# A transformer layer in float32 on one Trainium2 core: pool waits by tile, memory loads behind the first values, one more side block in front, query weights behind the last head

## The chip, the cores and the metric

The kernel runs on one core of one Trainium2 chip. The metric is the time of one execution in microseconds of the device (us); the time before is the median of three runs. The engines are named as the profile names them: PE (TensorE matmul), PEld (its weight loads), DVE (VectorE), ACT (ScalarE), POOL (GpSimd) and SP (SyncE, which here only issues DMAs).

## The reference

One layer over 1024 tokens of width 1024, with 256 memory tokens, in three residual steps. Norms are RMS norms.

```python
def parallel_mixer(xn, w_in, ...):
    proj = xn @ w_in
    fq, fk, fv, ff, gq, gk, gv, glr, gr = jnp.split(proj, _split_points(), axis=-1)
    ...
    fox_out = fox_attention(fq, fk, fv, log_f).reshape(B, S, FOX_WIDTH)      # 8 heads of 64
    ...
    return jnp.concatenate([fox_out, gla_out], axis=-1) @ w_out

def memory_cross_attention(hn, memn, wq, wkv, q_norm_g, k_norm_g, wo):       # 4 heads of 256
    q = rms_norm((hn @ wq).reshape(B, S, XATTN_HEADS, XATTN_HEAD_DIM), q_norm_g)
    k, v = jnp.split(memn @ wkv, 2, axis=-1)
    ...

h = h + parallel_mixer(rms_norm(h, norm_mix_g), ...)
h = h + memory_cross_attention(rms_norm(h, norm_xattn_g), rms_norm(mem, norm_mem_g), ...)
h = h + (jnp.square(jax.nn.relu(rms_norm(h, norm_mlp_g) @ mlp_w1))) @ mlp_w2
```

The forgetting attention (fox) is causal softmax attention over 8 heads with a bias from the running sum of log forget gates.

## The kernel before

Matrices are multiplied as two rounded parts each: a product is three matmuls (high times high, high times low, low times high), and `gemm` issues these three for each slice of 128 rows. `evac_split` makes the two parts of a PSUM bank: ACT writes the high part, DVE subtracts it for the low part. `wsplit` loads two slices of weights at a time into a `raw` tile (512 KB) and splits them, ACT for the high part `wh`, DVE for the low part `wl`.

The layer runs in stages. `mixer_inputs` makes the projections; its last loop makes the fox values, splits them and stores them tile by tile in DRAM (`vd`, L600). `fox` is the stage that the change touches. For each of 8 heads it loads the values of the head (`va`, L723), and for each of four pairs of query tiles `fox_scores` makes scores (`s`), a row maximum on DVE (`nm`), an exponential on ACT (`p`), a reciprocal on DVE (`rrec`) and a scaling on POOL (L671). `values` then transposes `p` in groups of up to four squares into one of three PSUM banks `tr` (L696), splits each group into `pth` (ACT) and `ptl` (DVE), and adds the products with the values into the one bank `pv` (L704). At the end of a pair `ol` (ACT, L707) and an add into `mixf` (DVE, L710) empty that bank. `fox_prep` loads the queries and keys of the next head (`qa`, `ka`, `qb`, `kb`).

Between these pieces a generator, `side_work`, puts work that depends on no head: eight blocks of the output projection's part for the gated linear attention (`out_part`: 12 matmuls into the one bank `mm`, then DVE adds the residual, `t2k`, L817, and stores it in `hpd`), the splitting of the memory's columns (`memr`, from `memT`), keys and values of the memory from the weights `wkv`, and eight blocks more of the output projection. `step` decides how many side pieces follow each pair of query tiles: 26 over the 32 pairs, after one ahead of the first. Then `project_out` ends the output projection, and `xattn` begins with the query weights (`weights(0)`, from `wq`).

A scheduler orders each engine's instructions from the dependencies and its own estimate of time, so a line's place in the program is a wish and not a place in a queue. `issue_after` adds a dependency: what is written under it is issued behind the named instruction. Each engine, SP too, works through its own instructions in order, so a waiting one holds those behind it. A DMA is issued with one of eight semaphores (`DMAHW0` to `DMAHW7`) in turn, and must wait until the earlier DMA of that semaphore has landed.

Pools reuse memory. A pool that is opened where another has been closed waits, at its first tile, for everything that used the memory before. With `reuse_waits="tile"` each tile waits only for what used the bytes of that tile. In `fox`, `foxpt` (the tiles `pth` and `ptl`) and `foxol` (`ol`) lie where the staging tiles `qn` of the values' loop lay.

Of the kernel before, what the change touches and what calls it, by code (L numbers as in the profile page):

```python
# [21 lines left out]
AF = mybir.ActivationFunctionType  # L22
ALU = mybir.AluOpType
# [7 lines left out]
P = 128  # L31
# [16 lines left out]
def f(ap):  # L48
    return ap.bitcast(F32)


class Layer:
# [52 lines left out]
    def gemm(self, ps, lh, ll, rh, rl, start=True, stop=True, **kw):  # L105

        mm = self.nc.tensor.matmul
        n = len(lh)
        for k in range(n):
            mm(ps, lh[k], rh[k], start=start and k == 0, stop=False, **kw)  # L110
            mm(ps, lh[k], rl[k], start=False, stop=False, **kw)  # L111
            mm(ps, ll[k], rh[k], start=False, stop=stop and k == n - 1, **kw)  # L112

# [564 lines left out]
    def fox(self):  # L678
        nc = self.nc
        with ExitStack() as st:  # L680
            pt = self.open(st, "foxpt", 5)
            olp = self.open(st, "foxol", 3)
            mmp = self.open(st, "mm2", 1, space=PSUM)
            pvp = self.open(st, "pv2", 1, space=PSUM)
            trp = self.open(st, "tr2", 3, space=PSUM)

            def values(h, sb, pp, A):
                va = A[4]
                pv = self.T(pvp, [P, 256], F32, "pv")
                for b in range(sb + 1):  # L690
# [10 lines left out]
                    self.evac_split(th[:, 0:n * P], tl[:, 0:n * P], tp[:, 0:n * P])  # L701
                    for j, w in ((0, th), (1, th), (1, tl), (0, tl)):
                        js = slice(j * 256, min((j + 1) * 256, n * P))
                        nc.tensor.matmul(pv[:, 256 - (js.stop - js.start):256], va[:, 2 * b + j, :], w[:, js],  # L704
                                         start=b == j == 0 and w is th, stop=b == sb and j == 0 and w is tl)
                ol = self.T(olp, [64, 256], F32, "ol")
                nc.scalar.activation(ol, pv[64:128, :], AF.Copy)  # L707
                o = self.mixf[(h % 2) * 64:(h % 2) * 64 + 64, 2 * sb:2 * sb + 2, h // 2, :]
                v3 = lambda ap: ap.rearrange("p (a b) -> p a b", a=2)
                nc.vector.tensor_tensor(o, v3(pv[0:64, :]), v3(ol), ALU.add)  # L710
                return first

            side = self.side_work(self.side, mmp, trp)
            prep = self.fox_prep
            next(side)
            A = self.fox_first

            def step(s):
                for _ in range(((s + 1) * 26 + 8) // 32 - (s * 26 + 8) // 32):
                    next(side, None)  # L720

            for h in range(8):
                nc.sync.dma_start(f(A[4]), self.vd[:, h])  # L723
                for g in range(2):
# [14 lines left out]
    def side_work(self, mp, mmp, trp):  # L739
# [11 lines left out]
        for t in range(2):  # L751
            xt = self.T(mp, [P, 4, M], F32, "memr", bufs=2)
            nc.sync.dma_start(xt, self.memT[:, 4 * t:4 * t + 4, :])
            for j in range(4):
                k, c = 4 * t + j, slice(2 * (j % 2), 2 * (j % 2) + 2)
                self.evac_split(mh[k // 2][:, c, :], ml[k // 2][:, c, :], xt[:, j, :].rearrange("p (t s) -> p t s", t=2), gm[:, k:k + 1])
            yield
# [4 lines left out]
        for n in range(4):  # L762
            W = self.wsplit(self.wkv[:, n * 512:(n + 1) * 512], None, rooms=mp)
            if n == 0:
# [34 lines left out]
    def out_part(self, mp, mmp, n, ks):  # L799
# [7 lines left out]
        for half in range(2):  # L807
# [3 lines left out]
            for i in range(4):  # L811
                ps = self.T(mmp, [P, 512], F32, "mm")
                c = slice(i * P, (i + 1) * P)
                self.gemm(ps, *([w[:, c] for w in w_] for w_ in W), *A)
                xt = self.T(mp, [P, 512], F32, "t2k", bufs=3)
# [154 lines left out]
    def xattn(self):  # L970
        nc = self.nc
        with ExitStack() as st:
# [16 lines left out]
            def weights(n):  # L989
                Ws[n] = self.wsplit(self.wq[:, n * 512:(n + 1) * 512], C_XAT)  # L990
                kT = self.T(kvp[n], [P, 2, 4, M], F32R, "kT")
# [367 lines left out]
```

## Time and profile before

| what | value |
|---|---|
| time, median of 3 runs | 1440.09 us (1438.77 to 1441.18) |
| the profiled execution | 1440.62 us |
| its span, first to last instruction | 1438.9 us |
| mean granted clock of PE | 0.998 |
| busy: PE, DVE, ACT, POOL | 99%, 65%, 47%, 27% of the span |
| DMA | 223.91 MB, mean 156 GB/s |
| the fox stage | about 325 to 550 us of the span |

A row of time has a start, a duration, engine, line, operation and tiles (out<-in); "xN" merges N neighbours of one kind, and a bracket gives the engine's idle time before the row and what ended it. A row of windows has the stretch, its length, busy time and count of PE, PEld, DVE, ACT and POOL, the granted clock, the share of DMA in use and GB/s. A row of waits reads: who waited for whom, us in total, times, longest.

### The profile page before, as it was taken

The numbers are of one execution on the slowest core, as the hardware profiler recorded it, in microseconds if no ns is written. First come the engines' busy times: TensorE is split into PE (matmuls) and PEld (weight loads), VectorE is DVE, ScalarE is ACT, GpSimd is POOL, SyncE is SP. The second block draws the span as 40 slices with busy tenths as digits, with TensorE's granted clock in tenths as the row PEclk, the third lists the DMA queues.
The fourth block names the chain that finished last, engine by engine and source line by source line (L and its number), as shares of the span: only waits on it lengthen the run. The fifth ranks groups of instructions, "written<-read, shape, count | busy, mean of one in ns | idle before, by whom it ended". The sixth has DMA issues, their size and how long they took to land.

```text
span 1438.9 us, 19147 instructions
## 1 busy us (share of the span) xinstructions
PE 1421.3 (99%) x7036; PEld 1185.4 (82%) x7036; DVE 937.8 (65%) x1342; ACT 675.2 (47%) x1095; POOL 385.2 (27%) x404
## 2 busy tenths in 40 slices
PE   9999999999999999999999999999999999999998
PEld 7788788887888887888888888888888888888887
DVE  5366732437887766666545895656556968778797
ACT  3544441336777655454532364444546745335230
POOL 3235423311333223412212300000000552233454
PEclk9999999999999999999999999999999999999999
DMA  8335530278678634322573124344446835436353
GB/s 313 92 65 140 130 79 0 74 190 285 173 193 239 177 110 148 124 74 90 171 273 140 44 95 179 145 168 190 176 175 231 320 107 190 134 133 217 123 191 124
DMA packets 121164, 223.91 MB, mean 156 GB/s; under 512 B 8912, under 2 KB 54512, under 8 KB 118512
## 3 DMA queue, kind: packets, MB, share of 16 engines
q1 hardware_dynamic: 119776, 218.25, 46.6%
q10 hardware_dynamic: 1296, 4.46, 1.0%
q8 instruction: 55, 0.90, 0.2%
q14 instruction: 37, 0.30, 0.1%
HBM read 150.59 MB, written 72.09 MB: 155 GB/s over the span
## 4 chain that ended last, share of the span: by engine, by line
PE 89%; DMA 4%; ACT 3%; DVE 2%; issue 2%; POOL 0%; SPq 0%; ACTq 0%; DVEq 0%; POOLq 0%
PE mm L110 15%; PE mm L111 15%; PE mm L112 15%; PE my L110 7%; PE my L112 7%; PE my L111 7%; PE tr L112 3%; PE tr L111 3%; PE tr L110 3%; PE pv L704 2%; PE tr L696 2%; PE s L660 1%; PE s L661 1%; DMA ud<-h 1%; DMA raw<-in_mlp_w_dram 1%
## 5 line engine op out<-in xcount | busy, mean ns | idle before, releaser
L110 PE MATMUL my<-x,g 128*128 128x512 f32 x464 | 180.7, 390 | 0.5 <-ACT h L1295 0.3
L111 PE MATMUL my<-x,g 128*128 128x512 f32 x464 | 180.6, 389 | 0.0
L112 PE MATMUL my<-x,g 128*128 128x512 f32 x464 | 180.5, 389 | 0.0
L111 PE MATMUL mm<-wl,xh 128*128 128x512 f32 x320 | 126.5, 396 | 0.6 <-DVE wl L100 0.6
L110 PE MATMUL mm<-wh,xh 128*128 128x512 f32 x320 | 125.9, 396 | 0.5 <-ACT wh L99 0.4
L112 PE MATMUL mm<-wh,xl 128*128 128x512 f32 x320 | 125.7, 393 | 0.0
L1087 ACT ACTIVATE g<-s 128x1024 fp32r<-128x1024 f32 (+1 forms) x72 | 69.0, 964 | 101.1 <-PE my L112 41.1
L1088 DVE TENSOR_TENSOR g<-raw,g 128x512 fp32r<-128x512 f32 (+3 forms) x72 | 69.2, 965 | 69.8 <-ACT g L1087 69.7
L1087 ACT ACTIVATE g<-raw 128x512 fp32r<-128x512 f32 (+3 forms) x72 | 55.5, 773 | 102.4 <-DMA raw<-in_mlp_w_dram 39.6
L110 PEld LDWEIGHTS my<-x,g 128*128 128x128 f32 x464 | 87.1, 188 | 19.5 <-ACT h L1295 0.7
L111 PEld LDWEIGHTS my<-x,g 128*128 128x128 f32 x464 | 87.1, 188 | 18.3 <-DVE x L1088 0.2
L1114 POOL TENSOR_TENSOR s<-raw 128x384 f32<-128x384 f32 (+1 forms) x20 | 26.5, 1324 | 282.1 <-DMA raw<-in_mlp_w_dram 254.5
L112 PEld LDWEIGHTS my<-x,g 128*128 128x128 f32 x464 | 87.1, 188 | 17.9
L671 POOL TENSOR_SCALAR p<-p,rrec 128x128 f32<-128x128 f32 (+3 forms) x64 | 52.8, 831 | 151.6 <-DVE rrec L670 143.1
L1088 DVE TENSOR_TENSOR g<-s,g 128x1024 fp32r<-128x1024 f32 (+1 forms) x72 | 86.6, 1205 | 9.0 <-ACT g L1087 9.0
L1257 DVE TENSOR_TENSOR x<-x 128x1024 fp32r<-128x1024 f32 (+1 forms) x64 | 77.0, 1223 | 17.6 <-ACT x L1256 17.3
L111 PE MATMUL mm<-x,g 128*128 128x512 f32 x220 | 85.7, 389 | 0.0
L110 PE MATMUL mm<-x,g 128*128 128x512 f32 x220 | 85.6, 389 | 0.0
L112 PE MATMUL mm<-x,g 128*128 128x512 f32 x220 | 85.6, 389 | 0.0
L110 PE MATMUL tr<-x,g 128*128 128x512 f32 x212 | 82.5, 389 | 0.0
L111 PE MATMUL tr<-x,g 128*128 128x512 f32 x212 | 82.5, 389 | 0.0
L112 PE MATMUL tr<-x,g 128*128 128x512 f32 x212 | 82.5, 389 | 0.0
(316 smaller groups left out, 3665.8 us busy)
## 6 DMA issues: line engine op xcount, KB each, us to landing
ud<-h SPq DMA_DIRECT2D x32, 768.0 KB
x<-ud SPq DMA_DIRECT2D x48, 512.0 KB
raw<-in_mlp_w_dram SPq DMA_DIRECT2D x20, 1024.0 KB
raw<-in_mlp_w_dram SPq DMA_DIRECT2D x16, 768.0 KB
raw<-in_w_in_dram SPq DMA_DIRECT2D x23, 512.0 KB
raw<-in_xattn_wkv_dram SPq DMA_DIRECT2D x16, 512.0 KB
od<-o SPq DMA_DIRECT2D x32, 256.0 KB
ud<-h SPq DMA_DIRECT2D x32, 256.0 KB
```

The lines of the kernel that those rows point to most:

```text
L110: mm(ps, lh[k], rh[k], start=start and k == 0, stop=False, **kw)
L111: mm(ps, lh[k], rl[k], start=False, stop=False, **kw)
L112: mm(ps, ll[k], rh[k], start=False, stop=stop and k == n - 1, **kw)
L660: nc.tensor.matmul(ps[:, c], qa[:, ts], ka[:, c], start=True, stop=False)
L661: nc.tensor.matmul(ps[:, c], qb[0:68, ts], kb[0:68, c], start=False, stop=not last)
L671: nc.gpsimd.tensor_scalar(p[:, 0:n], p[:, 0:n], rr, 1.0, ALU.mult, ALU.mult)
L696: t = nc.tensor.transpose(tp[:, c * P:(c + 1) * P], pp[i][:, (2 * b + j) * P:(2 * b + j + 1) * P], self.ident)
L704: nc.tensor.matmul(pv[:, 256 - (js.stop - js.start):256], va[:, 2 * b + j, :], w[:, js], start=b == j == 0 and w is th, stop=b == sb and j ...
L1087: a = self.nc.scalar.activation(hi, src, AF.Copy)
L1088: d = self.nc.vector.tensor_tensor(lo, src, f(hi), ALU.subtract)
L1114: eng.tensor_tensor(s[:, 0], raw[:, 3], raw[:, 2], ALU.add)
L1257: nc.vector.tensor_tensor(lo, f(lo), f(hi), ALU.subtract)
```

## The change

Four edits. `foxpt` waits by tile, and it is opened behind `foxol` instead of ahead of it. The loads of the memory's columns and of `wkv` are issued behind the load of the first head's values. Two pieces of side work instead of one are issued ahead of the heads, 25 instead of 26 follow with them, and the first head's first products with the values are issued behind the last matmul of the second side block. The loads and the splitting of the first query weights are written to be issued behind the last head's two closing instructions.

```diff
@@ gemm
-            mm(ps, ll[k], rh[k], start=False, stop=stop and k == n - 1, **kw)
+            end = mm(ps, ll[k], rh[k], start=False, stop=stop and k == n - 1, **kw)
+        return end.ins
@@ fox
-            pt = self.open(st, "foxpt", 5)
             olp = self.open(st, "foxol", 3)
+            pt = self.open(st, "foxpt", 5, reuse_waits="tile")
...
-                    for j, w in ((0, th), (1, th), (1, tl), (0, tl)):
...
+                    with ExitStack() as behind:
+                        if h == sb == 0:
+                            behind.enter_context(self.tc.issue_after(self.side_end))
+                        for j, w in ((0, th), (1, th), (1, tl), (0, tl)):
...
-                nc.scalar.activation(ol, pv[64:128, :], AF.Copy)
+                end = nc.scalar.activation(ol, pv[64:128, :], AF.Copy).ins
...
-                nc.vector.tensor_tensor(o, v3(pv[0:64, :]), v3(ol), ALU.add)
+                self.fox_end = end, nc.vector.tensor_tensor(o, v3(pv[0:64, :]), v3(ol), ALU.add).ins
...
-            next(side)
+
+            for _ in range(2):
+                next(side)
...
-                for _ in range(((s + 1) * 26 + 8) // 32 - (s * 26 + 8) // 32):
+                for _ in range(((s + 1) * 25 + 8) // 32 - (s * 25 + 8) // 32):
                     next(side, None)
...
-                nc.sync.dma_start(f(A[4]), self.vd[:, h])
+                self.va_load = nc.sync.dma_start(f(A[4]), self.vd[:, h]).ins
+                if h == 0:
+                    self.va_first = self.va_load
@@ side_work
-            nc.sync.dma_start(xt, self.memT[:, 4 * t:4 * t + 4, :])
+            with self.tc.issue_after(self.va_first):
+                nc.sync.dma_start(xt, self.memT[:, 4 * t:4 * t + 4, :])
...
-            W = self.wsplit(self.wkv[:, n * 512:(n + 1) * 512], None, rooms=mp)
+            with self.tc.issue_after(self.va_first):
+                W = self.wsplit(self.wkv[:, n * 512:(n + 1) * 512], None, rooms=mp)
@@ out_part
-                self.gemm(ps, *([w[:, c] for w in w_] for w_ in W), *A)
+                self.side_end = self.gemm(ps, *([w[:, c] for w in w_] for w_ in W), *A)
@@ xattn, weights(n)
-                Ws[n] = self.wsplit(self.wq[:, n * 512:(n + 1) * 512], C_XAT)
+
+                with self.tc.issue_after(self.fox_end[0]), self.tc.issue_after(self.fox_end[1]):
+                    Ws[n] = self.wsplit(self.wq[:, n * 512:(n + 1) * 512], C_XAT)
```

How it moves instructions, at three places. First ACT, at the first `pth` of the first head, with the semaphores that each instruction waits for; before:

```order
L668 ACTIVATE p_550_2952,rsum_2953<-s_548_2944,nm_2950 128x896 [waits DVE_49]
L117 ACTIVATE pth_2862<-tr_2858 128x384 [waits DMAHW6_49,PE_49,DMAHW7_49,Activation_49,Pool_49]
L117 ACTIVATE pth_2896<-tr_2891 128x512 [waits PE_49]
L117 ACTIVATE pth_2909<-tr_2904 128x512 [waits PE_49]
L668 ACTIVATE p_555_2964,rsum_2965<-s_553_2958,nm_2962 128x512 [waits DVE_49,Pool_49]
L117 ACTIVATE pth_2921<-tr_2917 128x384 [waits PE_49]
L88 ACTIVATE wh_3738<-raw_783_3736 128x512 [waits DMAHW1_49]
L88 ACTIVATE wh_3742<-raw_783_3736 128x512
L88 ACTIVATE wh_3748<-raw_3746 128x512 [waits DMAHW0_49]
L88 ACTIVATE wh_3752<-raw_3746 128x512
```

and in the changed kernel, where lines stand one or ten further down:

```order
L669 ACTIVATE p_552_2969,rsum_2970<-s_550_2961,nm_2967 128x896 [waits DVE_49]
L118 ACTIVATE pth_2879<-tr_2875 128x384 [waits PE_49,Activation_49,Pool_49]
L118 ACTIVATE pth_2913<-tr_2908 128x512 [waits PE_49]
L118 ACTIVATE pth_2926<-tr_2921 128x512 [waits PE_49]
L669 ACTIVATE p_557_2981,rsum_2982<-s_555_2975,nm_2979 128x512 [waits DVE_49,Pool_49]
L118 ACTIVATE pth_2938<-tr_2934 128x384 [waits PE_49]
L669 ACTIVATE p_562_2995,rsum_2996<-s_560_2987,nm_2993 128x1024 [waits DVE_49,Pool_49]
L669 ACTIVATE p_601_3142,rsum_3143<-s_599_3136,nm_3140 128x128 [waits DVE_49,Pool_49]
L711 ACTIVATE ol_2887<-pv_2874 64x256 [waits DMAHW7_49,DMAHW4_49,PE_49]
```

The first `pth` has lost its two DMA semaphores, and the first `ol` has gained two; in between, the splitting of `wkv` (L88) has left ACT's row.

Second SP, around the store of the last tile of values (`vd`) and the loads of the first two heads' values (`va`); before, from the second of two pieces of `wkv` on:

```order
L80 DMA raw_3766<-in_xattn_wkv_dram 128x2x512 [waits DMAHW1_49,DVE_49]
L746 DMA gxk_2788<-in_xattn_k_norm_g_dram 128x256 [waits DMAHW2_49,PE_49]
L816 DMA t2k_2840<-in_xT_dram 128x512 [waits DMAHW3_49]
L816 DMA t2k_2886<-in_xT_dram 128x512 [waits DMAHW4_49]
L816 DMA t2k_3026<-in_xT_dram 128x512 [waits DMAHW5_49]
L600 DMA vd_59<-qn_2758 1024x1x128 [waits DMAHW6_49,DVE_49]
L753 DMA memr_3576<-in_memT_dram 128x1024 [waits DMAHW7_49]
L753 DMA memr_3667<-in_memT_dram 128x1024 [waits DMAHW0_49]
L80 DMA raw_783_3736<-in_xattn_wkv_dram 128x2x512 [waits DMAHW1_49]
L80 DMA raw_793_3756<-in_xattn_wkv_dram 128x2x512 [waits DMAHW2_49]
L723 DMA va_2426<-vd_59 128x1024 [waits DMAHW6_49,DMAHW3_49]
L723 DMA va_2845<-vd_59 128x1024 [waits DMAHW4_49]
```

and in the changed kernel, from the store of the last tile but one on:

```order
L601 DMA vd_59<-qn_2729 1024x1x128 [waits DMAHW7_49,DVE_49]
L754 DMA gxk_2788<-in_xattn_k_norm_g_dram 128x256 [waits DMAHW0_49,PE_49]
L826 DMA t2k_2840<-in_xT_dram 128x512 [waits DMAHW1_49]
L826 DMA t2k_2857<-in_xT_dram 128x512 [waits DMAHW2_49]
L826 DMA t2k_2903<-in_xT_dram 128x512 [waits DMAHW3_49]
L601 DMA vd_59<-qn_2758 1024x1x128 [waits DMAHW4_49,DVE_49]
L729 DMA va_2426<-vd_59 128x1024 [waits DMAHW6_49,DMAHW7_49,DMAHW5_49,DMAHW4_49]
L729 DMA va_2862<-vd_59 128x1024
L762 DMA memr_3534<-in_memT_dram 128x1024
L762 DMA memr_3586<-in_memT_dram 128x1024 [waits DMAHW0_49]
```

The two `va` loads now stand right behind the last store; the two pieces of `wkv` that stood ahead of that store, and the memory's columns and two more pieces that stood ahead of the `va` loads, now come behind them.

Third DVE, at the end of the last head, where `wl` with `cols` is the query weights; before:

```order
L118 TENSOR_TENSOR ptl_5712<-tr_5706,pth_5711 128x512 [waits DVE_49,Activation_49]
L118 TENSOR_TENSOR ptl_5725<-tr_5719,pth_5724 128x512 [waits DVE_49,Activation_49]
L710 TENSOR_TENSOR mixf_2772<-pv_5653,ol_5679 64x2x128 [waits Activation_49]
L100 SCALAR_TENSOR_TENSOR wl_6155<-raw_6152,cols_74,wh_6154 128x512 [waits DMAHW7_49,Activation_49]
L100 SCALAR_TENSOR_TENSOR wl_6159<-raw_6152,cols_74,wh_6158 128x512 [waits Activation_49]
L118 TENSOR_TENSOR ptl_5738<-tr_5732,pth_5737 128x512 [waits DVE_49,Activation_49]
L118 TENSOR_TENSOR ptl_5750<-tr_5745,pth_5749 128x384 [waits Activation_49]
```

and in the changed kernel:

```order
L119 TENSOR_TENSOR ptl_5712<-tr_5706,pth_5711 128x512 [waits DVE_49,Activation_49]
L119 TENSOR_TENSOR ptl_5725<-tr_5719,pth_5724 128x512 [waits DVE_49,Activation_49]
L119 TENSOR_TENSOR ptl_5738<-tr_5732,pth_5737 128x512 [waits DVE_49,Activation_49]
L714 TENSOR_TENSOR mixf_2772<-pv_5653,ol_5679 64x2x128 [waits Activation_49]
L119 TENSOR_TENSOR ptl_5750<-tr_5745,pth_5749 128x384 [waits Activation_49]
L854 TENSOR_TENSOR sl_5829<-mixf_2772,sh_5828 128x512 [waits Activation_49]
L854 TENSOR_TENSOR sl_5969<-mixf_2772,sh_5968 128x512 [waits Activation_49]
L854 TENSOR_TENSOR sl_5973<-mixf_2772,sh_5972 128x512 [waits Activation_49]
L714 TENSOR_TENSOR mixf_2772<-pv_5705,ol_5757 64x2x128 [waits Activation_49]
L100 SCALAR_TENSOR_TENSOR wl_6155<-raw_6152,cols_74,wh_6154 128x512 [waits DMAHW7_49,Activation_49]
L100 SCALAR_TENSOR_TENSOR wl_6159<-raw_6152,cols_74,wh_6158 128x512 [waits Activation_49]
```

The first two pieces of the query weights stood between the low parts `ptl` of the last pair and now stand behind the last `mixf`; a `mixf` that stood ahead of two `ptl` now stands behind three.

More of the change, by code (lines that the diff above doesn't have):

```diff
@@ L701, in values @@
                     self.evac_split(th[:, 0:n * P], tl[:, 0:n * P], tp[:, 0:n * P])
-                    for j, w in ((0, th), (1, th), (1, tl), (0, tl)):
-                        js = slice(j * 256, min((j + 1) * 256, n * P))
-                        nc.tensor.matmul(pv[:, 256 - (js.stop - js.start):256], va[:, 2 * b + j, :], w[:, js],
-                                         start=b == j == 0 and w is th, stop=b == sb and j == 0 and w is tl)
+                    with ExitStack() as behind:
+                        if h == sb == 0:
+                            behind.enter_context(self.tc.issue_after(self.side_end))
+                        for j, w in ((0, th), (1, th), (1, tl), (0, tl)):
+                            js = slice(j * 256, min((j + 1) * 256, n * P))
+                            nc.tensor.matmul(pv[:, 256 - (js.stop - js.start):256], va[:, 2 * b + j, :], w[:, js],
+                                             start=b == j == 0 and w is th, stop=b == sb and j == 0 and w is tl)
                 ol = self.T(olp, [64, 256], F32, "ol")
-                nc.scalar.activation(ol, pv[64:128, :], AF.Copy)
+                end = nc.scalar.activation(ol, pv[64:128, :], AF.Copy).ins
                 o = self.mixf[(h % 2) * 64:(h % 2) * 64 + 64, 2 * sb:2 * sb + 2, h // 2, :]
                 v3 = lambda ap: ap.rearrange("p (a b) -> p a b", a=2)
-                nc.vector.tensor_tensor(o, v3(pv[0:64, :]), v3(ol), ALU.add)
+                self.fox_end = end, nc.vector.tensor_tensor(o, v3(pv[0:64, :]), v3(ol), ALU.add).ins
                 return first
```

## The prediction

> **What bounds the kernel now.** I read the busy shares first, then short windows, then the rows of time where TensorE (PE) stands still.
>
> ```profile
> PE 1421.3 (99%) x7036; PEld 1185.4 (82%) x7036; DVE 937.8 (65%) x1342; ACT 675.2 (47%) x1095; POOL 385.2 (27%) x404
> 325.00:335.00 10.00, 6.65 (x34) 4.80 (x34) 6.72 (x13) 5.69 (x14) 1.57 (x2) 0.94 1.00 343
> 335.00:540.00 205.00, 202.61 (x1215) 172.39 (x1215) 160.45 (x316) 138.82 (x310) 60.94 (x76) 0.99 0.64 188
> 540.00:550.00 10.00, 7.81 (x51) 6.61 (x50) 9.94 (x18) 8.19 (x16) 0.00 (x0) 1.00 0.55 187
> ```
>
> PE is the bound: 1421.3 of 1438.9 us. An edit can win only where PE is idle or slow. The three windows are the forgetting-attention heads (their entry, body and end); columns are length, then busy time of PE, PEld, DVE, ACT, POOL, granted clock, DMA share, GB/s. PE is idle 3.35 us in the entry, 2.39 in 205 us of body, 2.19 in the end. That is 7.9 us; a clock loss comes on top:
>
> ```profile
> 331.33 0.23 PE L663 MATMUL s<-maskb,identb 128*128 128x128 bf16 x1
> 333.57 1.47 ACT L117 ACTIVATE pth<-tr 128x384 fp32r<-128x384 f32 x3 [4.31 <-DMA vd<-qn]
> 334.80 0.87 PE L696 MATMUL tr<-ident,p 128*128 128x128 f32 x3 [3.24 <-DVE ptl L118]
> 333.50:334.00 0.50, 0.00 (x0) 0.00 (x0) 0.00 (x0) 0.42 (x2) 0.00 (x0) 0.71 1.06 414
> 334.00:340.00 6.00, 5.11 (x15) 3.97 (x16) 5.90 (x11) 5.02 (x11) 0.69 (x1) 0.50 1.04 391
> 340.50:341.00 0.50, 0.50 (x3) 0.38 (x2) 0.00 (x0) 0.50 (x3) 0.00 (x0) 0.96 0.84 148
> ```
>
> PE ends a score at 331.56 and needs a fourth bank for transposes. Three exist; the first is emptied by pth (ACT) and ptl (DVE), and ACT's pth waits 4.31 us for the last store of the values, vd<-qn, to land. Nothing in pth reads vd: it is a wait on reused memory. PE idles 3.24 us, and 2.2 us into that the clock falls to half, to 340.5. Some 5.7 us of work at half clock cost 2.8 us more. So the entry loses 6.0 us.
>
> **The change, part by part.**
>
> *Pool waits by tile, and the two pools swapped.* The order shows that the first pth no longer waits for any DMA. Its wait has gone to ol, which comes behind the first value product pv and so behind a load that needs those stores anyway: cost nothing. What is late next is DVE, and with it the one bank of the side blocks:
>
> ```profile
> 329.07 0.20 ACT L668 ACTIVATION_READ_ACCUMULATOR p<-s,nm 128x1 f32 x1
> 330.15 0.67 DVE L665 TENSOR_REDUCE nm<-s 128x1 f32<-128x512 f32 x1
> 334.10 1.18 DVE L118 TENSOR_TENSOR ptl<-tr,pth 128x384 fp32r<-128x384 f32 x2 [3.28 <-ACT pth L117]
> 335.19 0.68 DVE L817 TENSOR_TENSOR t2k<-mm,t2k 128x512 f32<-128x512 f32 x1
> ```
>
> ACT ends its exponential at 329.27, where pth can now start instead of 333.57. DVE is free at 330.82; two ptl and the add that frees the bank then end at 330.82 + 1.2 + 0.7 = 332.7. PE meanwhile has three transposes, a score and one transpose (0.1 a transpose and 0.6 a score, by the rows below): 331.56 + 1.0 = 332.6. So the second side block starts at 332.8.
>
> *One more side block in front, and the first pv issued behind it.* A block is twelve matmuls. At full clock:
>
> ```profile
> 341.24 0.93 PE L696 MATMUL tr<-ident,p 128*128 128x128 f32 x7
> 341.92 0.43 PE L704 MATMUL pv<-pth,va 128*128 128x256 f32 x2
> 342.46 0.40 PE L660 MATMUL s<-ka,qa 128*128 128x512 f32 x1
> 343.57 0.47 PE L110 MATMUL mm<-sh,wh 128*128 128x512 f32 x1
> 346.42 0.49 PE L696 MATMUL tr<-ident,p 128*128 128x128 f32 x3
> ```
>
> The block from 343.57 to 346.42 took 2.85 us, so PE reaches pv at 335.65. Before, too, PE did a second block ahead of pv, at half clock: this edit only secures the cover. Behind pv come pv itself (0.54, from 341.92 to 342.46), seven transposes (0.68) and two scores (1.11): the third block starts at 337.98, where before it started at 343.57. **Entry: 5.6 us**, less what PE waits for the values at 335.65.
>
> *Memory loads behind the first values.* This decides that wait. The queue of SP before:
>
> ```profile
> 324.27 1.85 SPq L816 DMA_DIRECT2D t2k<-in_xT_dram  x3
> 326.23 0.53 SPq L600 DMA_DIRECT2D vd<-qn  x1
> 326.80 1.56 SPq L753 DMA_DIRECT2D memr<-in_memT_dram  x2
> 333.46 0.81 SPq L723 DMA_DIRECT2D va<-vd  x2
> 339.78 0.28 SPq L645 DMA_DIRECT2D qb<-cq  x1
> SPq L645 <- DMA va<-vd: 0.8, 1, 0.8
> ```
>
> The store was issued at 326.23 and landed at 333.4. The load va followed at 333.46 and landed at 339.75, as the L645 behind it, which waited for that load, shows: 7.2 and 6.3 us. Loads of 512 KB with little else in flight took 3.7 to 4.75:
>
> ```profile
> 37.39 4.75 DMA xt<-in_x_dram
> 154.70 3.71 DMA raw<-in_w_in_dram
> DMA packets 281, 0.14 MB, mean 288 GB/s; under 512 B 0, under 2 KB 281, under 8 KB 281
> DMA packets 101, 0.19 MB, mean 373 GB/s; under 512 B 9, under 2 KB 11, under 8 KB 101
> DMA packets 319, 0.18 MB, mean 355 GB/s; under 512 B 2, under 2 KB 309, under 8 KB 319
> DMA packets 50, 0.20 MB, mean 393 GB/s; under 512 B 1, under 2 KB 1, under 8 KB 50
> ```
>
> The packet rows are half microseconds from 289.0 (a lone store: 281 of its 512-byte packets), 328.0, 329.5 and 332.5. This store had hardly begun at 328, ran at the lone rate at 329.5 and was over at 332.5. So it was held by what was issued ahead of it: two wkv pieces (which now go behind va), gxk and three xT pieces (which stay). The memory loads behind it may have stretched its tail; they and two more wkv pieces, 2 MB, then stood ahead of va. Bounds for the store now: 329.9 (326.23 + 3.7) to 333.4. I take 331.5, near the middle, since gxk and xT still stand ahead. For va, bounds are 3.7 and 6.3; with nothing ahead I take 4.2, the mean of the two rows. That gives 335.7, bounds 333.6 to 339.7. PE waits 0.1 us by the middle values; I charge 0.4. **Entry: 5.2 us.**
>
> The Trainium skill, "DMA: Bandwidth & Descriptors", section "Queues, rings and completion order", speaks against the memory loads as a cause: descriptors of one issuing engine are consumed in ring order on each DMA engine, so loads issued behind a store do not pass it. By that rule alone, the store could gain only from the wkv pair; the packet rows agree for its bulk and leave its last microsecond open. The result is the first rival.
>
> What the loads now meet: memory columns and wkv are needed some blocks later. In ACT's queue the first wkv conversion moves behind the second pth of the next group, some 344. Its piece is issued once the next head's query load has landed: behind 2.5 MB, which at the 391 GB/s of the window from 334 take 6.4 us after 331.5, and 2.4 us of latency (3.71 less 1.3 for the bytes), so at 340.3, and lands at 344. PE needs the pth behind that conversion some 11 us after the third block's start, at 349 (two blocks 5.7, two pv groups 2.4, 17 transposes 1.7, a score 0.9). That is the cover: cost nothing; the third rival has the rest.
>
> *The heads' body.* Every step of side work comes one block earlier and the order changes throughout, though no instruction is added. The largest stall of the body:
>
> ```profile
> 425.00:430.00 5.00, 3.87 (x29) 3.33 (x29) 4.97 (x11) 3.85 (x10) 4.92 (x4) 1.00 1.05 254
> 428.41 0.55 PE L696 MATMUL tr<-ident,p 128*128 128x128 f32 x3 [1.13 <-POOL p L671]
> ```
>
> The 1.13 us came from POOL doing two rstd steps ahead of a score's scaling; the new order puts that scaling between them. Against it, POOL now does both memory rows' factors ahead of a scaling. Bounds: 1.1 won to 4 lost; I take 0, since 2.4 us in 205 is what such an order lost before.
>
> *Query weights behind the last head.* DVE bounds the end (9.94 of 10 us):
>
> ```profile
> 544.40 0.55 PE L696 MATMUL tr<-ident,p 128*128 128x128 f32 x3 [1.22 <-DVE ptl L118]
> 545.43 1.41 DVE L100 SCALAR_TENSOR_TENSOR wl<-raw,cols,wh 128x512 fp32r<-128x512 f32 x2
> 545.45 0.51 PE L704 MATMUL pv<-pth,va 128*128 128x256 f32 x2 [0.50 <-DVE mixf L710]
> 546.76 1.15 DVE L118 TENSOR_TENSOR ptl<-tr,pth 128x512 fp32r<-128x512 f32 x2
> 547.49 0.51 PE L704 MATMUL pv<-ptl,va 128*128 128x256 f32 x2 [0.47 <-DVE ptl L118]
> 550.00:555.00 5.00, 5.00 (x24) 4.14 (x23) 1.48 (x3) 0.00 (x0) 0.00 (x0) 1.00 0.54 153
> ```
>
> PE waits 1.22 + 0.50 + 0.47 = 2.19 us here. Two query conversions (1.41 us) stood ahead of the last ptl; behind the heads they fall where DVE is busy 1.48 us of 5 and ACT not at all: hidden. Were that cover gone, three conversions would cost about 2.1 us. PE's order also changes: a group of pv now splits the last side block, so that DVE runs ahead meanwhile. Late next is mixf: it frees the one pv bank and stands behind three ptl now (1.8 us by 546.76), against one pv group of 0.9 on PE. I leave 1.0 us of the 2.19. **End: 1.2 us**, bounds 0 to 2.2.
>
> **Sum.** 5.2 + 0 + 1.2 = 6.4 us. The profiled execution took 1440.62 us (span 1438.9), 0.53 over the median of the three runs shown, 1440.09. 1440.62 - 6.4 = 1434.2, as a median 1433.7. Beyond 550 us the orders agree but for a few neighbours, and PE is full in the window from 550.
>
> **The rivals.**
>
> *The store lands no earlier.* For it: only the wkv pair ahead of it goes, and DMA was full from 328. Then va lands at 333.4 + 4.2 = 337.6, PE waits 2.0 us, the entry gives 3.6 and the sum is 4.8: 1435.3. PE's clock fell 2.2 us into the idle time before, so this is at the edge of another 2.8 us: 1438.1. The Trainium skill, "TensorE: Matmul & The Clock Gate", section "Why this matters for your kernels", allows gaps up to about 3 us; here 2.2 sufficed, so the trace is less lenient. By that rule the 2.8 would not fall due.
>
> *The body gives back.* POOL's new order, or a later scaling, stalls PE a few times by the size of 428.41; 4 us lost leaves 2.4: 1437.7. For it: DVE is 78% busy there (160.45 of 205). Against: the old order lost only 2.4 in all.
>
> *Slower: ACT's queue blocks on wkv.* The first wkv conversion waits in ACT's queue ahead of a pth. If its piece lands after 347 (349 less two conversions and the pth), PE waits for it one to one, beyond 2.2 us with 2.8 more for the clock. To be slower by over 0.2% (9.3 us lost), it must land after 353.5, against an issue at 340.3. The longest wait for one DMA in the chain is 9.7 us:
>
> ```profile
> 1136.05 9.69 DMA ud<-h
> ```
>
> So 13.2 is hardly reached; then 1443.
>
> *The change not doing what it says* (pth still waiting for the store) is excluded by the order.
>
> **How the numbers follow.** Forecast 0.62; store no earlier 0.20; body gives back 0.14; ACT blocked 0.04. The measurement tells about 0.2% (2.9 us) from no change. Faster: the forecast, most of the store's case and a little of the body's, 0.83. Within 0.2%: the rest of those, 0.13. Slower 0.04. Low end: no wait for va, the end's whole 2.2 and the POOL stall gone, 5.6 + 2.2 + 1.1 = 8.9: 1431.2, rounded to 1431. High end: both middle rivals at their worse prices, 1438.
>
> **What would show it.** Right: the first pth near 329.3 with no wait for vd, the clock at 1.00 from 330 to 345, the first pv between 335.6 and 336.5, the third side block near 338, and ptl with no query conversion before it at the end. Wrong: a wait of over 2 us of PE on va with a clock of 0.50, a row of ACT waiting for in_xattn_wkv, or more than 4 us of idle PE in the body.

## The result, and the profile after

| | before | after |
|---|---|---|
| time, median (runs) | 1440.18 us (4) | 1449.97 us (4: 1447.51, 1449.90, 1450.03, 1450.37) |
| ratio, 95% interval | | 1.0068 (1.0055 to 1.0080) |
| profiled execution, span | 1440.62, 1438.9 us | 1447.51, 1445.8 us |

The change makes the kernel 0.7% slower. The ratios in the tables compare undisturbed runs of both kernels on one chip, so they need not be the quotients of the medians.

The same stretches of both kernels, as windows (length, busy time of PE, PEld, DVE, ACT and POOL, granted clock, DMA share, GB/s); first before:

```profile
325.00:345.00 20.00, 16.56 (x77) 12.78 (x77) 15.49 (x30) 13.05 (x29) 4.09 (x5) 0.83 1.02 329
345.00:365.00 20.00, 20.00 (x124) 17.11 (x123) 15.20 (x33) 11.72 (x29) 4.45 (x6) 1.00 0.68 214
365.00:540.00 175.00, 172.70 (x1050) 147.29 (x1049) 136.48 (x266) 119.74 (x265) 53.98 (x67) 1.00 0.61 178
540.00:560.00 20.00, 17.81 (x95) 14.89 (x94) 13.30 (x23) 9.75 (x19) 0.00 (x0) 1.00 0.48 150
```

And after:

```profile
325.00:345.00 20.00, 19.85 (x115) 16.03 (x114) 16.38 (x34) 12.93 (x30) 5.02 (x7) 1.00 0.85 264
345.00:365.00 20.00, 12.53 (x57) 9.64 (x56) 12.14 (x25) 10.29 (x23) 2.49 (x3) 0.74 0.85 277
365.00:540.00 175.00, 170.71 (x1040) 145.97 (x1040) 133.45 (x264) 117.84 (x260) 50.75 (x67) 1.00 0.62 181
540.00:560.00 20.00, 17.83 (x109) 15.31 (x108) 16.42 (x26) 12.30 (x24) 1.13 (x1) 1.00 0.37 119
352.60:362.84 10.24, 5.56 (x15) 3.96 (x16) 9.21 (x20) 7.22 (x18) 1.78 (x3) 0.50 0.86 286
```

Idle time of PE is the length less its busy time. From 325 to 345 it falls from 3.44 to 0.15 us, and the clock stays at 1.00: with the 2.8 us that the half clock cost before, 6.1 us are won (the third side block starts 5.35 us earlier). From 345 to 365 it rises from nothing to 7.47, and in the last row PE works 5.56 us at half clock, which costs 2.8 more: 10.3 us lost. The body loses 4.29 instead of 2.30, so 2.0 more; the end loses 2.17 instead of 2.19. That is 6.2 us of the 6.9 between the two spans. The rest is small: idle time differs by +0.9 ahead of 325, +0.3 from 560 to 860 and -0.3 behind, where the orders agree but for neighbours. A second reading agrees: each profile has 7036 matmuls of PE, and the 2930th, in the first work behind the heads, starts at 560.56 us before and at 567.17 after, 6.6 later.

So the entry went as planned, and a new stall right behind it took more than it gave. The entry first, in the timeline of the changed kernel (start, duration, engine, line, tiles; lines below 700 move by up to 4):

```profile
326.27 0.52 SPq L601 DMA_DIRECT2D vd<-qn  x1
332.01 0.81 SPq L729 DMA_DIRECT2D va<-vd  x2
343.20 1.03 SPq L80 DMA_DIRECT2D raw<-in_xattn_wkv_dram  x2
329.45 1.46 ACT L118 ACTIVATE pth<-tr 128x384 fp32r<-128x384 f32 x3
335.76 0.45 PE L708 MATMUL pv<-pth,va 128*128 128x256 f32 x2
338.22 0.48 PE L110 MATMUL mm<-sh,wh 128*128 128x512 f32 x1
```

The first `pth` waits for nothing, the first product `pv` comes at 335.76 with no wait for `va`, and the third side block starts at 338.22 instead of 343.57. Then the stall:

```profile
343.10 1.09 ACT L118 ACTIVATE pth<-tr 128x512 fp32r<-128x512 f32 x2
349.60 1.15 ACT L88 ACTIVATE wh<-raw 128x512 fp32r<-128x512 f32 x2 [5.41 <-DMA raw<-in_xattn_wkv_dram]
350.66 0.58 ACT L118 ACTIVATE pth<-tr 128x512 fp32r<-128x512 f32 x1
...
353.21 1.69 ACT L121 ACTIVATE sh<-memr,cols 128x256 fp32r<-128x256 f32 x4
353.28 0.95 DVE L666 TENSOR_REDUCE nm<-s 128x1 f32<-128x768 f32 x1
...
356.25 0.90 ACT L669 ACTIVATE p<-s,nm 128x768 f32<-128x768 f32 x1
352.21 0.33 PE L697 MATMUL tr<-ident,p 128*128 128x128 f32 x1 [2.73 <-DVE ptl L119]
357.28 0.79 PE L661 MATMUL s<-ka,qa 128*128 128x512 f32 x1 [4.74 <-ACT p L669]
```

ACT had done two of the three `pth` of a group when the next instruction in its queue, the first wkv conversion, had to wait 5.41 us for its piece, issued at 343.20. The third `pth` came at 351 and PE went on at 352.21, only to stop again: behind that `pth` ACT had three more conversions, two parts of `mixg` and four of the memory's columns to do before the exponential `p` for which PE waited 4.74 us. DVE stood in the same way, so `p`'s row maximum `nm` came at 353.28 and ended at 354.23: up to there DVE's queue would have held `p` as well, from there to 356.25 only ACT's own work did.

### The profile page after: what moved, and what is told of

Its sections match the earlier page's. It is cut to its first block, busy times and chain, and to the rows that moved or that the text cites. A ratio compares the mean times of both kernels' runs of the same rounds, so it can differ in the third digit from the quotient of the medians.

```text
span 1445.8 us, 19164 instructions
## 1 busy us (share of the span) xinstructions
PE 1421.1 (98%) x7036; PEld 1185.4 (82%) x7036; DVE 941.4 (65%) x1342; ACT 675.0 (47%) x1095; POOL 380.5 (26%) x404
## 4 chain that ended last, share of the span: by engine, by line
PE 88%; DMA 4%; ACT 3%; DVE 2%; issue 2%; SPq 0%; POOL 0%; ACTq 0%; DVEq 0%; POOLq 0%
PE mm L110 14%; PE mm L111 14%; PE mm L112 14%; PE my L110 7%; PE my L112 7%; PE my L111 7%; PE tr L112 4%; PE tr L111 4%; PE tr L110 4%; PE pv L708 2%; PE tr L697 1%; PE s L661 1%; PE s L662 1%; DMA qa<-qd 1%; DMA xt<-in_x_dram 1%
```

## The experiments

Four theories; the fourth was added when conv_late had run. **Q**: a conversion that waits for its load in an in-order queue holds what PE needs. **T** (traffic): what PE needs itself lands late, whatever ACT's order. **O**: the new order of the side work costs the time. **L**: what stands ahead of a load in SP's queue decides. The columns by stretch are the idle time of PE in us, from the windows of each profile. The next one is how long the clock was at half between 325 and 900 us, which costs half of PE's busy time in it. The last compares the start of the 2930th matmul with the kernel before, in us:

| kernel | median us | ratio to before (95%) | 325-345 | 345-365 | 365-540 | 540-560 | half clock | 2930th |
|---|---|---|---|---|---|---|---|---|
| before | | 1 | 3.44 | 0 | 2.30 | 2.19 | 6.83 | 0 |
| after | 1449.97 | 1.0068 (1.0055-1.0080) | 0.15 | 7.47 | 4.29 | 2.17 | 10.24 | +6.61 |
| conv_late | 1442.09 | 1.0004 (0.9993-1.0015) | 0.15 | 4.33 | 2.69 | 1.72 | 6.83 | +1.43 |
| wkv_free | 1442.24 | 1.0015 (1.0004-1.0025) | 1.99 | 1.13 | 2.67 | 1.76 | 3.41 | +0.15 |
| mem_free | 1444.49 | 1.0025 (1.0015-1.0036) | 0.46 | 3.63 | 2.55 | 1.71 | 3.41 | +1.47 |
| both_free | 1440.94 | 1.0000 (0.9991-1.0008) | 3.33 | 0 | 2.35 | 1.77 | 6.83 | +1.19 |
| pools_alone | 1440.58 | 1.0005 (0.9994-1.0016) | 3.55 | 0 | 2.31 | 1.72 | 6.83 | +0.41 |
| wkv_behind_xt6 | 1442.48 | 1.0011 (1.0000-1.0022) | 0.15 | 0 | 5.88 | 1.72 | 6.83 | +0.37 |
| wkv_behind_va3 | 1444.14 | 1.0022 (1.0013-1.0032) | 1.04 | 0 | 6.11 | 1.72 | 10.24 | +4.43 |
| xt6_old_query | 1442.12 | 1.0018 (1.0008-1.0028) | 0.14 | 0.09 | 5.30 | 2.32 | 0 | -0.97 |
| xt4_conv_free | 1445.92 | 1.0037 (1.0024-1.0050) | 0.50 | 3.75 | 3.70 | 1.76 | 3.41 | +3.39 |
| xt4_conv_late | 1441.33 | 1.0007 (0.9997-1.0016) | 0.17 | 0.85 | 5.15 | 1.75 | 0 | -0.43 |
| wkv_free_conv_late | 1442.77 | 1.0018 (1.0009-1.0026) | 2.27 | 0 | 3.95 | 1.76 | 3.41 | +1.95 |
| wkv_split_loads | 1444.94 | 1.0024 (1.0014-1.0035) | 0.15 | 0.17 | 6.27 | 1.76 | 0 | +0.32 |

All edits are made to the changed kernel, but for `pools_alone`.

**conv_late.** The loads stay, the first block's conversions go behind a later `pth` (`splits` collects what `evac_split` returns in `values`):

```diff
-            with self.tc.issue_after(self.va_first):
+            with ExitStack() as behind:
+                for ins in (self.va_first, *(self.splits[13] if n == 0 else ())):
+                    behind.enter_context(self.tc.issue_after(ins))
```

> All loads stay as in the changed kernel; the conversions of the first wkv block are queued behind the fourth pth of head two (in the profile of the changed kernel the first of them began at 349.6 us, here at about 360). Theory Q (ACT's queue: a conversion waits for its piece ahead of a pth that PE needs): no row of ACT waits for wkv over 0.5 us, PE is full from 335 to 365 at clock 1.00, the 7.5 us of idle PE and about 2.8 us of half clock go: 1436 us (1434 to 1439). Theory T (traffic: DMA is full from 333 to 361, so what PE needs comes late whatever ACT's order): PE still idles over 4 us between 345 and 365, on a load of the next head or a value load: 1444 or more. Theory O (the new order of the side work costs the time): PE idles over 6 us somewhere in 335 to 540: 1444 or more.

It took 8 us less than the changed kernel, but 6 more than Q had it: PE still idled 4.33 us from 345 to 365, and the clock was at half for 6.83 us. Its timeline:

```profile
348.88 0.35 SPq L829 DMA_DIRECT2D t2k<-in_xT_dram  x1
356.35 0.69 DVE L830 TENSOR_TENSOR t2k<-mm,t2k 128x512 f32<-128x512 f32 x1 [5.92 <-DMA t2k<-in_xT_dram]
357.10 0.80 PE L110 MATMUL mm<-sh,wh 128*128 128x512 f32 x1 [3.86 <-DVE t2k L830]
```

No conversion stops ACT now, and a second wait shows that it had covered: the residual's piece (`xT`) for the fourth side block is issued at 348.88, behind all four wkv pieces, and lands at 356.3. DVE's add waits for it, and with it the one bank `mm` and the `ptl` behind the add. This is no traffic that PE reads itself, as T had it, but L: a small load behind 2 MB. In the changed kernel the same piece was issued at 347.74.

**wkv_free, mem_free, both_free.** One or both of the two `issue_after(self.va_first)` are taken out.

```diff
-            with self.tc.issue_after(self.va_first):
-                W = self.wsplit(self.wkv[:, n * 512:(n + 1) * 512], None, rooms=mp)
+            W = self.wsplit(self.wkv[:, n * 512:(n + 1) * 512], None, rooms=mp)
```

> Only wkv's loads are no longer put behind the first value load: two pieces are issued near 319.6 and two near 326.8 again, as before the change; the memory loads stay behind the values. Theory Q: the conversions end by 337 as before the change and the stall at 349 to 362 goes; the last store of the values has two more pieces ahead of it, so the first pv is later than 335.8, by 0 to 3 us: 1437 us (1435 to 1440). Theory T: the same bytes in all, so the stall moves but stays over 4 us: 1444 or more. Theory O: 1444 or more.

> Only the memory loads are no longer put behind the first value load (they are issued ahead of it again); wkv stays behind it. The order of ACT's queue now has the first wkv conversion one pth earlier (ahead of the second group's first pth), and its piece is issued right behind the value loads, at about 333, ahead of head two's tiles. Theory Q: that piece lands near 340, PE needs that pth at 341 and waits 0 to 3 us; the third piece, issued behind head two's query tile (about 343), lands near 349 ahead of a pth needed near 349.5, so PE waits 0 to 3 us again; no wait of 7 us: 1439 us (1435 to 1444). Theory T: as the changed kernel, 1447 or more. Theory O: 1444 or more.

> Neither the memory loads nor wkv's are put behind the first value load; pool waits by tile, the side block in front and the query conversions behind the last head stay. Theory Q: no stall at 349; the last store of the values lands near 333.4 and the first value load near 339 as before the change, so PE, which reaches the first pv at 335.7, waits about 3 us there and may lose 2.8 more to the clock: 1438 us (1436 to 1441). Theory T: 1440 or less, too. Theory O (the order costs it): 1444 or more.

With wkv free there is no stall at 349, as Q says, and the order (O) is not what cost it. But the conversions, back between the first group's `pth`, delay an exponential, and `va` has 1 MB ahead. PE in that kernel:

```profile
336.38 0.38 PE L661 MATMUL s<-ka,qa 128*128 128x256 f32 x1 [0.97 <-ACT p L669]
337.22 0.44 PE L708 MATMUL pv<-pth,va 128*128 128x256 f32 x2 [0.21 <-DMA va<-vd]
338.37 0.50 PE L661 MATMUL s<-ka,qa 128*128 128x512 f32 x1 [0.42 <-ACT p L669]
```

Three short waits, and the clock fell to half from 339.10 to 342.51; 1442.2 is above the expected range. In mem_free (1444.5, half a microsecond above its range, with a wait of PE of 3.53 us where 3 at most were expected) the first conversions came in time, and a later one did what the first does in the changed kernel:

```profile
351.60 0.63 ACT L88 ACTIVATE wh<-raw 128x512 fp32r<-128x512 f32 x1 [4.09 <-DMA raw<-in_xattn_wkv_dram]
355.33 0.63 PE L708 MATMUL pv<-pth,va 128*128 128x256 f32 x2 [3.53 <-DVE mixf L714]
```

In both_free the memory loads and half of wkv stand ahead of `va` as before the change, and PE waits for `va`:

```profile
340.13 0.69 PE L708 MATMUL pv<-pth,va 128*128 128x256 f32 x2 [3.18 <-DMA va<-vd]
```

The store, `vd`, took 5.80 us there from its issue (326.89) to the load that waits for it (332.69), with 2 MB of loads issued behind it; with the same behind it, it took 7.23 before and 6.26 in pools_alone, and with no load issued between the two it took 5.74 in the changed kernel and 5.62 to 7.02 in seven others. The Trainium skill, "DMA: Bandwidth & Descriptors", section "Queues, rings and completion order", has descriptors consumed in ring order on each DMA engine, though a later one may finish its write before an earlier one. The runs agree in so far as no dependence on the loads behind the store shows: its time scatters alike with and without them. The two wkv pieces ahead of the store, which stand there in both_free too, do not decide it either. So what the change won at the entry by its loads is in `va`, which had 2 MB less ahead of it: it was issued at 332.69 and reached PE at 340.13 in both_free, at 332.01 and 335.76 in the changed kernel.

**pools_alone.** The kernel before with the first edit only.

```diff
-            pt = self.open(st, "foxpt", 5)
             olp = self.open(st, "foxol", 3)
+            pt = self.open(st, "foxpt", 5, reuse_waits="tile")
```

> The kernel before with one edit of the change only: pool waits by tile and the two pools swapped. Theory L: the first pth starts near 329 and PE runs on to 335.7, but the first value load still stands behind 2 MB of memory and wkv loads and lands near 340, so the wait on the store is replaced by a wait on that load of 3 us and its clock loss: 1440.5 us (1439 to 1442). Rival P (the store's wait alone cost the 6 us): 1435 us (1433.5 to 1437).

Measured 1440.58, no change that can be told. The wait on the store is gone and one on the load stands in its place:

```profile
329.44 1.46 ACT L117 ACTIVATE pth<-tr 128x384 fp32r<-128x384 f32 x3
339.99 0.45 PE L704 MATMUL pv<-pth,va 128*128 128x256 f32 x2 [3.40 <-DMA va<-vd]
```

So the pools' edit does not pay without the loads out of the way, and the loads out of the way are what stalls PE later. The loads moved without the pools' edit were not run.

**xt4_conv_free, xt4_conv_late.** Now the piece that conv_late waited for goes ahead of wkv, once with the conversions where the order puts them, once with them late. This parts Q from L.

```diff
-            with self.tc.issue_after(self.va_first):
+            with ExitStack() as behind:
+                for ins in (self.xt_loads[3],):
+                    behind.enter_context(self.tc.issue_after(ins))
```

(`xt_loads` collects the `xT` loads of `out_part`; the second kernel adds `self.splits[13]` as above.)

> wkv's loads go behind the fourth xT piece, so that piece (the one the run with late conversions waited for) is ahead of them; the conversions of wkv stand where the order puts them, the first one still ahead of the last pth of head one. Theory Q (a conversion waiting in ACT's queue stops PE): the first piece is issued near 348 and lands near 353, ACT waits over 4 us for it, and PE idles 3 to 7 us between 348 and 362, though the xT piece is there in time: 1444 us (1441 to 1450). Rival X (the xT piece behind 2 MB was the whole cause, and ACT's wait harmless): PE idles under 1 us from 345 to 365: 1439 us or less.

> The same loads as xt4_conv_free, but the conversions of the first wkv block stand behind the fourth pth of head two, as in conv_late. Theory Q with L (both queues matter): PE idles under 1.5 us from 335 to 365 and the 5.3 us of the entry are kept at 365; the body's order is close to that of wkv_behind_xt6 and gives back about 4 us between 380 and 510, as there: 1439 us (1435 to 1443). Rival X: the same time as xt4_conv_free.

The first, in its timeline:

```profile
351.80 1.15 ACT L88 ACTIVATE wh<-raw 128x512 fp32r<-128x512 f32 x2 [4.77 <-DMA raw<-in_xattn_wkv_dram]
352.46 1.29 DVE L93 TENSOR_TENSOR wl<-raw,wh 128x512 fp32r<-128x512 f32 x2 [4.70 <-ACT wh L88]
353.68 0.68 DVE L831 TENSOR_TENSOR t2k<-mm,t2k 128x512 f32<-128x512 f32 x1
354.42 0.54 PE L110 MATMUL mm<-sh,wh 128*128 128x512 f32 x1 [3.75 <-DVE t2k L831]
```

The `xT` piece is there (the add at 353.68 waits for nothing), but in DVE's queue it stands behind the low part of a conversion, which waits for ACT, which waits for wkv: PE stops 3.75 us. With the conversions late the stall shrinks to 0.85 us, and the kernel is 0.3% faster, with intervals that do not meet. Both expectations held; Q and L are both at work.

**wkv_behind_xt6, wkv_behind_va3, wkv_free_conv_late, wkv_split_loads.** Four attempts to keep the entry's gain, by other places for loads and conversions; the edit of each, in this order (`va_third` is the value load of head three):

```diff
-            with self.tc.issue_after(self.va_first):
+                for ins in (self.xt_loads[5], *(self.splits[15] if n == 0 else ())):
...
+                for ins in (self.va_third, *(self.splits[17] if n == 0 else ())):
...
+                for ins in self.splits[13] if n == 0 else ():
...
+                for ins in self.splits[13] if n == 0 else ():
...
+                W = self.wsplit(..., late=self.xt_loads[4] if n == 0 else None)
@@ wsplit, in the last
+                if late is not None and k0 % 4 == 0:
+                    behind.enter_context(self.tc.issue_after(late))
```

> wkv's loads go behind the sixth xT piece (issued near 357 in the run with late conversions) instead of behind the first value load, and the first block's conversions behind the sixth pth of head two. Theory L (what is queued ahead of it decides: 2 MB of wkv pieces, issued from 343 to 348, stand ahead of the xT piece that a side block's add needs, and ahead of their own conversions' need): no idle time of PE over 1 us from 335 to 365, clock 1.00 from 330 to 365, so the entry's 5.3 us stay won: 1435.5 us (1433 to 1438). Rival B (bunch: the conversions, now queued side by side ahead of head two's later pth, stop PE over 2 us between 365 and 395): 1438 to 1441. Rival N (the whole gain of the entry is eaten by the new order of the body, wherever wkv stands): 1440 or more, with PE idle over 6 us from 365 to 640.

> wkv's loads go behind the value load of head three (issued near 363), ahead of head three's query and key tiles; the first block's conversions behind the eighth pth of head two, some 10 us before PE uses them. Theory L: no idle time over 1 us from 335 to 365 either; head three's tiles have 2 MB more ahead of them, but are needed 15 us later: 1436 us (1433.5 to 1439). Rival B: the conversions end after PE needs them at about 390, and PE idles 2 to 5 us between 380 and 400: 1438 to 1441. Rival N: 1440 or more.

> wkv's loads ahead of the values as before the change (two near 319.6, two near 326.5), the memory loads behind them, the first block's conversions behind the fourth pth of head two. Theory Q with L: nothing of wkv stands ahead of the fourth xT piece or of a pth; the first value load has 1 MB of wkv ahead and lands near 337.2, so PE waits 1.5 us there with or without a loss of clock (0 to 1.7), and nothing until 365; the body gives back about 4 us: 1440 us (1436 to 1443).

> Two of the four pieces (those whose buffers are free early) are issued near 319.6 as before the change, the other two behind the fifth xT piece; conversions behind the fourth pth of head two. Theory L: the first value load lands by 335.8 and PE does not wait for it, nor for an xT piece: under 1 us idle from 330 to 365; the body gives back about 4 us: 1438.5 us (1434 to 1442). If the body gives back as much here too, with its conversions ready 5 us earlier than in wkv_behind_xt6, its loss comes from the order and not from late loads.

The first and the last have both stretches, 325 to 345 and 345 to 365, clean: 0.32 us of idle PE at most, against 3.44 and a clock loss before. Still none beats the kernel before, and three of the four came out above their ranges (wkv_free_conv_late alone within): from 365 to 540 they idle 3.95 to 6.27 us instead of 2.30, in wkv_behind_va3 with 10.24 us of half clock on top, in wkv_behind_xt6 with 3.41. By the 2930th matmul the first and the last have given back all that they had won (0.37 and 0.32 us behind), and more is lost later: at the first `tr<-ident,qn`, 32 us on, they are 2.1 and 2.2 behind. The two kernels that led at the 2930th (xt4_conv_late by 0.43, xt6_old_query by 0.97) are 0.7 and 0.4 behind there. The table's idle times of the heads alone do not show this part. The largest wait of wkv_behind_xt6 near 380:

```profile
381.05 1.06 ACT L137 ACTIVATE memr<-memr 128x1024 f32<-128x1024 f32 x1 [2.09 <-DMA memr<-in_mem_dram]
382.11 0.58 ACT L799 ACTIVATE t2k<-mm 128x512 f32<-128x512 f32 x1
382.74 0.50 PE L110 MATMUL mm<-wh,sh 128*128 128x512 f32 x1 [1.68 <-ACT t2k L799]
```

It is the same pattern a third time: the copy that frees PE's bank stands behind an instruction that waits for a memory row. wkv_split_loads, which loads half of the first block early, gives back as much, and ACT waits there for a later wkv piece and for the same memory row:

```profile
376.72 0.63 ACT L91 ACTIVATE wh<-raw 128x512 fp32r<-128x512 f32 x1 [2.40 <-DMA raw<-in_xattn_wkv_dram]
381.88 1.06 ACT L140 ACTIVATE memr<-memr 128x1024 f32<-128x1024 f32 x1 [2.21 <-DMA memr<-in_mem_dram]
```

PE then waits 1.56 us for the copy behind them. So late loads and the queues' order are not told apart in the body; which wait belongs to which reordering was not separated.

**xt6_old_query.** wkv_behind_xt6 without the last edit of the change.

```diff
-                with self.tc.issue_after(self.fox_end[0]), self.tc.issue_after(self.fox_end[1]):
-                    Ws[n] = self.wsplit(self.wq[:, n * 512:(n + 1) * 512], C_XAT)
+                Ws[n] = self.wsplit(self.wq[:, n * 512:(n + 1) * 512], C_XAT)
```

> As wkv_behind_xt6, but the query weights are converted where the order puts them, as before the change. The prediction's term for the end, 1.2 us: this kernel is 1.2 us slower than wkv_behind_xt6, with 2.2 us of idle PE between 540 and 550 against 1.0. Rival: the runs so far show 1.7 us of idle PE at the end with the edit, so it is worth 0.5 us, within the noise.

PE idles 2.32 us at the end instead of 1.72, so the edit is worth 0.6 there, near the rival's 0.5 and half of the term's 1.2; in the times (1442.12 against 1442.48, overlapping intervals) it cannot be told.

## Why the prediction was wrong

Predicted were 6.4 us won; the profiled executions show 6.9 lost.

*The entry (5.2) was right.* Second block 332.8 predicted, 332.82 measured; first `pv` 335.65 and 335.76; third block 337.98 and 338.22; store landed 331.5 and 332.0, no wait for `va`, clock at 1.00. Part of it was luck: the step had the store gain from the wkv pieces that no longer stand ahead of it, but with them ahead it landed as soon in both_free (5.80 us), and in wkv_behind_va3, without them, it took 7.02 and PE waited 0.90 for `va`. So the rival of a store that lands no earlier was open in each execution, and did not come in this one.

*The step that failed* is the cover for wkv in the part on the memory loads: "at 340.3, and lands at 344. PE needs the pth behind that conversion some 11 us after the third block's start, at 349 ... That is the cover: cost nothing". The need was right: PE ran out at 349.5. The landing was wrong twice. The piece was issued at 343.20, when head two's query tile had landed, and its data came 6.4 us later, where 3.7 was taken. The changed kernel's windows while SP's queue worked off the values, the memory and head two's tiles, and while the piece was under way, and the next two:

```profile
333.00:343.00 10.00, 10.00 (x60) 8.52 (x61) 6.70 (x16) 4.58 (x12) 3.44 (x5) 1.00 1.00 316
343.00:349.60 6.60, 6.48 (x42) 5.47 (x40) 1.71 (x3) 1.17 (x3) 0.00 (x0) 1.00 1.02 293
...
345.00:350.00 5.00, 4.48 (x29) 3.65 (x27) 0.02 (x1) 0.40 (x1) 0.00 (x0) 1.00 1.00 290
350.00:355.00 5.00, 0.33 (x1) 0.14 (x1) 4.74 (x8) 5.00 (x12) 0.00 (x0) 0.76 1.05 397
```

The issue was late mostly by a rate: DMA was full, but at 316 GB/s and not at the 391 of the window taken. At that rate the 2.5 MB take 7.9 us and not 6.4, the store landed 0.5 later, and 0.9 of the 2.9 us stays open. The landing was late by a term that is missing: 3.7 us is the time of a load with little else in flight, but in the 6.6 us from 343.00 to 349.60 the queue moved 1.94 MB, of which the piece is 0.5. The rest was ahead of it or beside it: what was left of head two's tiles (by the size of the packets, an estimate, 0.6 MB) and, for the most part, the wkv pieces issued right behind. From 345 to 350 ACT and DVE stood still (0.40 and 0.02 of 5 us) while PE lived on what was done.

*The rival "ACT's queue blocks on wkv" had the place and the mechanism, and the wrong price.* It let PE wait one to one for the landing: with a landing at 349.6 that makes 2.6 us, against the 2.73 of PE's first wait, and so it put the point of "slower" at a landing of 353.5, "hardly reached". With 2.8 for the clock that price is 5.4 us, against 10.3 measured. For ACT's work does not vanish while it waits. The row of 350 to 355 shows ACT at 5.00 of 5 and DVE at 4.74: the conversions, the memory's parts and then the exponential came in one row, and PE waited 4.74 us more for the last of them. And a second load, the `xT` piece, stood behind the same 2 MB, though no row of the changed kernel waits for it; conv_late shows that it alone holds PE 3.86 us, xt4_conv_free that a conversion alone holds it 3.75. The chance of 0.04 rested on a price that took only the landing.

*The body (0, between 1.1 won and 4 lost)* lost 2.0, within its bounds. The stall near 428 did not go; it grew, and PE now waits there for ACT's exponential and not for POOL's scaling. A new one came:

```profile
428.99 0.50 PE L661 MATMUL s<-ka,qa 128*128 128x512 f32 x1 [1.80 <-ACT p L669]
474.46 0.50 PE L110 MATMUL mm<-sh,wh 128*128 128x512 f32 x1 [1.03 <-ACT t2k L788]
```

*The end (1.2)* gave nothing in this order: 2.17 us of idle PE against 2.19 (0.6 in wkv_behind_xt6, by xt6_old_query). The step named `mixf` as late next and left 1.0 us for it; it took all:

```profile
550.55 0.51 PE L708 MATMUL pv<-pth,va 128*128 128x256 f32 x2 [1.34 <-DVE mixf L714]
552.91 0.50 PE L708 MATMUL pv<-pth,va 128*128 128x256 f32 x2 [0.83 <-DVE mixf L714]
```

*Open:* three of the four timed runs took 2.4 to 2.9 us more than the profiled one; no trace shows where. What most of these kernels lose in the first 32 us behind the heads was not followed up. That no arrangement beats the kernel before is shown for those tried only.

## What to carry to other kernels

A load that is moved back is needed where its first reader stands in an in-order queue, not where its data is used: here PE first read the memory's weights at 384 us, but their conversion stood ahead of a `pth` without which PE ran out of work. Look up that place on each engine, and the place of every small load that falls behind the moved bytes in the DMA queue. And price such a block by the landing plus all the work queued up to what the bound engine needs, since a stopped engine still has that to do.

## What the runs showed of the hardware

Short waits took the clock too. In wkv_free no gap of PE was over 0.97 us (the three rows above), yet:

```profile
335.70:339.10 3.40, 2.10 (x11) 1.63 (x11) 3.37 (x9) 2.99 (x7) 0.93 (x2) 1.00 0.99 347
339.10:342.51 3.41, 3.41 (x15) 2.92 (x14) 2.16 (x5) 2.04 (x6) 0.98 (x2) 0.50 0.99 298
```

PE was busy 2.10 of 3.40 us, and the next 3.41 us ran at half clock. The half-clock phase was 10.24 us in the changed kernel and 3.41 here, three to one to within 0.01 us. Phases within one execution also start whole multiples of 3.413 us apart: at 340.52 and 545.32 in pools_alone (60 of them), at 423.83 and 509.17 in wkv_behind_va3 (25). The Trainium skill, "TensorE: Matmul & The Clock Gate", section "What's actually happening", has a free-running window of about 3.4 us by which the clock is decided; lengths and starts agree.

The Trainium skill, "TensorE: Matmul & The Clock Gate", section "Why this matters for your kernels", allows gaps up to about 3 us. Here gaps of 0.97, 0.21 and 0.42 us, in or just ahead of one such window, were enough. The longest gap does not decide, and PE's busy share as the profile models it does not alone:

```profile
420.42:423.83 3.41, 2.36 (x11) 1.44 (x10) 3.35 (x7) 3.33 (x9) 2.39 (x2) 1.00 1.00 270
423.83:427.24 3.41, 3.41 (x13) 3.19 (x14) 3.17 (x8) 1.99 (x5) 1.26 (x4) 0.50 1.01 279
731.02:734.43 3.41, 1.78 (x16) 1.57 (x14) 1.98 (x3) 2.01 (x5) 0.00 (x0) 1.00 0.71 219
```

The first two rows are wkv_behind_va3, where no gap was over 0.45 us, PE was 69% busy and the clock fell; the last is mem_free, where PE waited 2.02 us (1.63 of it in this window), was 52% busy, and the clock stayed at 1.00 in the next. With all fourteen traces cut at the starts of these windows, a fall followed each of the 10 windows in which PE was at most 50% busy (those already at half clock left out), 4 of 36 between 50% and 70%, and none of the others.
